# Attention scores with the rotary keys' two halves stacked, and softmax scaling moved into the transposing matmul

## The chip, the cores and the metric

The kernel runs on one core of a Trainium2 chip. The metric is the device time of one execution in microseconds, given as the median of several runs. Five engines work side by side: TensorE (PE; its weight loads are listed apart as PEld), VectorE (DVE), ScalarE (ACT), GpSimd (POOL) and SyncE (SP, which here only issues transfers). TensorE writes to PSUM, where eight banks of 128 partitions by 512 fp32 values are used in turn; DVE and ACT read them out.

## The reference

Two layers run over 256 latent and 256 context tokens with 1024 features. Each layer has a SwiGLU feed-forward block, a token mixer and a second feed-forward block. The mixer of the first layer is a short convolution, that of the second is multi-head latent attention, and only that one is touched here:

```python
def latent_attention(q, k_all, v_all):        # 8 heads, 256 latent queries, 512 keys
    ...
def softmax_attend(q, k, v):
    s = jnp.einsum("bhqd,bhkd->bhqk", q, k).astype(jnp.float32) * QK_SCALE
    p = jax.nn.softmax(s, axis=-1).astype(v.dtype)
    return jnp.einsum("bhqk,bhkd->bhqd", p, v)
```

Queries and keys have 192 features in each head: 128 plain ones ("nope") and 64 rotary ones, which carry a rotation by position. The rotary part of a key is the same for all heads but for a factor of the head's normalisation.

## The kernel before

All activations and weights are fp32. To multiply with nearly full precision, each operand is split into a rounded high part (type fp32r, made on ACT by a cast, `split`, L210) and a low part (the rest, made on DVE by a subtraction, L211), and a product takes three matmuls: high by high, high by low, low by high. The helper `mm3` (L200 to L202) does this for the weights. In the attention stage the names are `q` and `qr` for the plain and the rotary queries (views of the tiles `arh` and `arl`, high and low, which also hold the transposed compressed queries `cqT` and the compressed keys `ckT`), `kt` for a pair of heads' keys (a pair of tiles `wh`, `wl` from the pool of weight slots), `pts` for transposed probabilities (also `wh`, `wl`), `vv` for the values (`vyh`, `vyl`) and `ot` for the output.

The code is traced in a program order, and a scheduler then fixes one static instruction list for each engine. Each engine works through its list in order, with semaphores between engines. The attention stage's program order comes from a hand-written string of steps (`MLA_ORDER`) and then a loop over i = 0 to 15 (8 heads by 2 blocks of 128 queries). The parts that matter:

- `q_norm`, `q_out` (steps N and O, once for each block of 128 tokens): the rotation of the queries in rows (`rot`, on DVE and POOL), then transposes on TensorE (L874) of three tiles of 128 by 512: two with the plain parts of four heads each, `tn`, and one with the rotary parts of all eight heads, `tr`. Two heads' rotary parts share a 128-wide transpose, so a head's 64 rotary features land on partitions 0 to 63 or 64 to 127. Each transposed tile is split by ACT and DVE (L210, L213 on ACT; L211, L214 on DVE).
- `kv_mm` (L916 to L918): compressed keys times the weights `kv`, for keys (step K) and values (step V). `k_pair` normalises the keys and writes plain parts to `kn` (DVE, L940) and rotary parts to `h` (POOL, L945).
- `keys(j)` for heads 2j and 2j+1: 12 transposes on TensorE (L997), eight of `kn` and four of `h`, and three splits.
- `scores(i)`: six matmuls into one PSUM bank, three over 128 plain features (L1012 to L1014) and three over 64 rotary features (L1015 to L1017, 64 rows of the array); then the row maximum on DVE (L1020), the exponential with a row sum on ACT (L1023), the reciprocal on DVE (L1024), and on DVE the scaling of the 128 by 512 probabilities `p` (L1025).
- `probs(i)`: four transposes of `p` (L1035) against the unit matrix (`cst`), and a split.
- `values(hd)`: twelve matmuls (L1046 to L1048) and a split to `ot`.

In the loop, `scores` runs two steps ahead of `probs`, and `keys` for the next pair of heads stands three steps ahead of its first use. A transpose is one pass through the array; a normal matmul of fp32 operands (not fp32r) takes two, each with its own weight load, and shows as two instructions in the profile. The normalisation's `norm_stats` (L361, L362) and the first layer's `mod_rows` (L284) already use such fp32 matmuls; L284 places four of them side by side in the columns of the array (`tile_position`, 32 columns each). The output projection's weights are converted (`conv_raw`, L178 on ACT and L179 on DVE) during the last steps of the loop.

```python
def split(self, src, h, l, scale=None):
    if scale is None:
        self.nc.scalar.copy(h, src)                                              # L210, ACT
        self.nc.vector.tensor_tensor(l, src, h.bitcast(F32), ALU.subtract)       # L211, DVE
```

Of the kernel before, what the change touches and what calls it, by code (L numbers as in the profile page):

```python
# [15 lines left out]
P = 128  # L16
# [60 lines left out]
class Kern:  # L77
# [578 lines left out]
    def sumsq(self, src, nh, w, out, scale=1.0):  # L656
        nc = self.nc
        for i in range(nh):
            j = self.tmp.tile([P, T], F32, tag="t2", name=self.nm("sj"), bufs=1)
            nc.scalar.activation(  # L660
                j[:, :w], src[:, i * w:(i + 1) * w], AF.Square, scale=scale, accum_out=out[:, i:i + 1]
            )
# [14 lines left out]
    def mla(self, l, nxt, mp):  # L677
# [9 lines left out]
        qr = [t[:, nq:nq + nq // 2].rearrange("p (h t) -> p h t", h=HEADS // 2) for t in (arh, arl)]  # L687
        b = nq + nq // 2
        cqT = [t[:, b:b + 2 * NLAT].rearrange("p (k t) -> p k t", k=2) for t in (arh, arl)]
        ckT = [t[:, b + 2 * NLAT:b + 2 * NLAT + T] for t in (arh, arl)]  # L690
        kn = mp.tile([P, 4, HEADS * P], F32, tag="kn", name="kn")
        krr = self.cst[:, P:].rearrange("p (t r) -> p t r", t=4)
# [163 lines left out]
        def q_norm(tt):  # L856
# [10 lines left out]
            return src[:1] + [(t, qr, 0, None)] + src[1:]  # L867

        def q_out(tt, src):
            ts = slice(tt * P, (tt + 1) * P)  # L870
            for t, dst, h0, g in src:
                tp = self.mmps()
                for i in range(4):
                    nc.tensor.transpose(tp[:, i * P:(i + 1) * P], t[:, i * P:(i + 1) * P], self.ident)  # L874
# [111 lines left out]
        kts, pts, ps = {}, {}, {}  # L986

        def keys(j):
            kts[j] = kt = self.wslot()
            for i in range(3):  # L990
                tp = self.mmps()
                for tt in range(4):
                    if i < 2:
                        src = kn[:, tt, (2 * j + i) * P:(2 * j + i + 1) * P]
                    else:
                        src = self.h[:, 2 * tt + j // 2, NLAT + (j % 2) * P:NLAT + (j % 2 + 1) * P]
                    nc.tensor.transpose(tp[:, tt * P:(tt + 1) * P], src, self.ident)  # L997
                s = slice(i * T, (i + 1) * T)
                self.split(tp, kt[0][:, s], kt[1][:, s])

        def scores(i):
# [3 lines left out]
            sl = slice(e * hp, (e + 1) * hp)  # L1005
            ns = slice(e * T, (e + 1) * T)
            rs = slice(2 * T, 3 * T)
# [3 lines left out]
            qp = [t[sl, j, qs] for t in qr]  # L1011
# [3 lines left out]
            mm(S, qp[0], kt[0][sl, rs], start=False, stop=False)  # L1015
            mm(S, qp[0], kt[1][sl, rs], start=False, stop=False)  # L1016
            mm(S, qp[1], kt[0][sl, rs], start=False, stop=True)  # L1017
# [7 lines left out]
            nc.vector.tensor_scalar(p, p, st[:, 2:3], None, ALU.mult)  # L1025
# [341 lines left out]
```

## Time and profile before

| | |
|---|---|
| median of 3 runs | 1633.65 us (1632.89 to 1637.13) |
| the profiled execution's own time, and its span | 1631.98 us, 1630.2 us |
| TensorE busy | 1599.2 us (98%), 8747 matmuls |
| DVE busy, ACT busy, POOL busy | 1113.4 us (68%), 586.1 us (36%), 58.6 us (4%) |
| transfers | 245.32 MB, mean 150 GB/s |
| attention stage | about 1288 to 1413 us of the span |

How to read it: the timeline has a row for each run of like instructions, with the start in the span, the time from the first start to the last end, engine, line, operation, the tiles (output and inputs), the shape and the count; in brackets stands the idle time before it and who ended that. Matmuls are pipelined, so one starts before the last has ended: what a matmul costs on TensorE is the distance from its start to the next one's start, not its own duration. The list of waits gives who waited for whom, total us, how often, and the longest.

### The profile page before, as it was taken

The page shows a single profiled execution, that of the slowest core. Times are in us where ns is not written, and L with a number is a line of the kernel's source. Part 1 is how long each engine was busy: PE and PEld are TensorE (multiplying, and loading weights), DVE is VectorE, ACT ScalarE, POOL GpSimd, SP SyncE. Part 2 cuts the span into 40 slices and gives each one's busy share as a digit, 9 for nine tenths or more (in the row PEclk, how much of TensorE's full clock was granted, in tenths as well). Part 3 has the DMA queues.
Part 4 walks back from the last instruction along what each step waited for, and adds up shares of the span by engine and source line. Part 5 has one row for each costly group of instructions (what it writes and reads, how often), then busy time and mean ns, then how long its engine had stood idle before and what let it go on. Part 6 is the DMA issues. An engine that isn't in the chain of part 4 may idle for free.

```text
span 1630.2 us, 21844 instructions
## 1 busy us (share of the span) xinstructions
PE 1599.2 (98%) x8747; PEld 1374.0 (84%) x8747; DVE 1113.4 (68%) x1967; ACT 586.1 (36%) x915; POOL 58.6 (4%) x69
## 2 busy tenths in 40 slices
PE   5999999999999999999999999999999998999999
PEld 4888888889888898888888898888888976899999
DVE  4568666676897678766666677767665678885553
ACT  4622222224423352222232352132223465664442
POOL 0000000001000200000000200000000211000000
PEclk9999999999999999999999999999999999999999
DMA  9545444431354425444444425444432120245553
GB/s 361 187 158 194 161 161 168 167 143 67 140 194 169 154 78 183 166 165 146 181 149 148 143 80 191 161 159 160 166 142 102 61 78 1 82 174 200 181 193 104
DMA packets 48677, 245.32 MB, mean 150 GB/s; under 512 B 5440, under 2 KB 6720, under 8 KB 33216
## 3 DMA queue, kind: packets, MB, share of 16 engines
q1 hardware_dynamic: 48576, 243.94, 41.6%
q8 instruction: 68, 1.11, 0.3%
q14 instruction: 33, 0.27, 0.1%
HBM read 242.87 MB, written 1.05 MB: 150 GB/s over the span
## 4 chain that ended last, share of the span: by engine, by line
PE 93%; DVE 4%; ACT 1%; DMA 1%; issue 0%; SPq 0%; POOL 0%; DVEq 0%; ACTq 0%
PE mm L200 30%; PE mm L202 30%; PE mm L201 29%; DVE nt L378 0%; PE mm L1035 0%; PE mm L1015 0%; DMA h<-hT 0%; PE mm L284 0%; PE mm L1046 0%; DMA raw<-wukv 0%; DVE nu L383 0%; DVE yl L384 0%; PE mm L1047 0%; PE mm L1016 0%; PE mm L1048 0%
## 5 line engine op out<-in xcount | busy, mean ns | idle before, releaser
L200 PE MATMUL mm<-yh,wh 128*128 128x512 f32 (+1 forms) x1674 | 596.7, 357 | 4.6 <-ACT wh L1209 2.5
L201 PE MATMUL mm<-yh,wl 128*128 128x512 f32 (+1 forms) x1674 | 595.2, 356 | 0.4 <-DVE wl L1211 0.3
L202 PE MATMUL mm<-yl,wh 128*128 128x512 f32 (+1 forms) x1674 | 594.3, 356 | 0.1
L178 ACT CAST wh<-raw 128x1024 fp32r<-128x1024 f32 (+4 forms) x348 | 319.1, 941 | 617.7 <-PE mm L202 508.4
L179 DVE TENSOR_TENSOR wl<-raw,wh 128x1024 fp32r<-128x1024 f32 (+4 forms) x348 | 377.6, 1103 | 47.1 <-ACT wh L178 45.3
L200 PEld LDWEIGHTS mm<-yh,wh 128*128 128x128 f32 x1674 | 316.6, 189 | 51.4 <-ACT yh L382 3.1
L201 PEld LDWEIGHTS mm<-yh,wl 128*128 128x128 f32 x1674 | 316.8, 189 | 45.3 <-DVE wl L1211 0.9
L202 PEld LDWEIGHTS mm<-yl,wh 128*128 128x128 f32 x1674 | 316.1, 189 | 45.2 <-DVE yl L384 0.3
L260 DVE CUSTOM_DVE_ANT_0 junk<-wm,crow 128x1024 f32<-128x1024 f32 x256 | 316.0, 1234 | 3.9
L200 PE MATMUL mm<-gh,wh 128*128 128x512 f32 (+1 forms) x848 | 294.9, 348 | 0.0
L202 PE MATMUL mm<-gl,wh 128*128 128x512 f32 (+1 forms) x848 | 294.4, 347 | 0.0
L201 PE MATMUL mm<-gh,wl 128*128 128x512 f32 (+1 forms) x848 | 294.2, 347 | 0.0
L455 DVE TENSOR_TENSOR s<-mm,s 128x512 f32<-128x512 f32 (+1 forms) x86 | 54.1, 629 | 249.7 <-PE mm L202 240.8
L202 PEld LDWEIGHTS mm<-gl,wh 128*128 128x128 f32 x848 | 160.5, 189 | 20.5 <-DVE gl L211 0.5
L200 PEld LDWEIGHTS mm<-gh,wh 128*128 128x128 f32 x848 | 160.5, 189 | 20.2
L201 PEld LDWEIGHTS mm<-gh,wl 128*128 128x128 f32 x848 | 160.5, 189 | 20.2
L402 DVE SCALAR_TENSOR_TENSOR h<-mm,fin,h 128x256 f32<-128x256 f32 x192 | 88.7, 478 | 122.7 <-PE mm L202 122.7
L454 ACT ACTIVATE s<-mm 128x512 f32<-128x512 f32 (+1 forms) x86 | 47.2, 548 | 189.9 <-PE mm L202 189.7
L211 DVE TENSOR_TENSOR gl<-s,gh 128x512 fp32r<-128x512 f32 (+1 forms) x86 | 53.5, 622 | 2.1 <-ACT gh L210 2.1
L210 ACT CAST gh<-s 128x512 fp32r<-128x512 f32 (+1 forms) x86 | 48.7, 566 | 6.5 <-DVE s L455 6.5
L346 ACT ACTIVATE sq<-h 128x256 f32<-128x256 f32 (+1 forms) x50 | 25.4, 507 | 69.9 <-DVE h L402 68.3
L382 ACT ACTIVATE yh<-nt,fin 128x256 fp32r<-128x256 f32 x66 | 36.5, 595 | 33.7 <-DVE nt L378 31.9
(215 smaller groups left out, 962.5 us busy)
## 6 DMA issues: line engine op xcount, KB each, us to landing
raw<-w SPq DMA_DIRECT2D x101, 1024.0 KB, 4.8
wm<-wmod SPq DMA_DIRECT2D x132, 512.0 KB, 3.7
raw<-w SPq DMA_DIRECT2D x32, 896.0 KB, 4.6
raw<-cin_cu SPq DMA_DIRECT2D x8, 1024.0 KB, 4.8
early<-wmod SPq DMA_DIRECT2D x12, 512.0 KB, 8.9
raw<-cin_b SPq DMA_DIRECT2D x8, 512.0 KB, 3.5
raw<-cout SPq DMA_DIRECT2D x4, 1024.0 KB, 4.8
raw<-wo SPq DMA_DIRECT2D x4, 1024.0 KB, 4.9
```

The lines of the kernel that those rows point to most:

```text
L178: self.nc.scalar.copy(h[:, b0:b1], raw[:, b0:b1])
L179: self.nc.vector.tensor_tensor(l[:, b0:b1], raw[:, b0:b1], h[:, b0:b1].bitcast(F32), ALU.subtract)
L200: mm(o, wh[:, b], xh[:, k, c[0]:c[1]], start=start, stop=False)
L201: mm(o, wl[:, b], xh[:, k, c[0]:c[1]], start=False, stop=False)
L202: mm(o, wh[:, b], xl[:, k, c[0]:c[1]], start=False, stop=stop)
L210: self.nc.scalar.copy(h, src)
L211: self.nc.vector.tensor_tensor(l, src, h.bitcast(F32), ALU.subtract)
L260: ins = nc.vector.tensor_tensor_reduce(junk, w, self.crow[:, cond, :], 1.0, 0.0, ALU.mult, ALU.add, o)
L382: nc.scalar.activation(yh, t, AF.Identity, bias=sh, scale=a)
L402: self.nc.vector.scalar_tensor_tensor(hh, ps[:, lo:hi], self.f(l, j, d, cond), hh, ALU.mult, ALU.add)
L454: nc.scalar.activation(s[:, :w], p1[:, :w], AF.Silu)
L455: nc.vector.tensor_tensor(s[:, :w], p3[:, :w], s[:, :w], ALU.mult)
```

## The change

- Keys: for each head its own tile of rotary keys is made, with the high part on partitions 0 to 63 and the low part on partitions 64 to 127. To have the same 64 features on both halves of the partitions, `keys` no longer transposes `h`: the new helper `twice` multiplies a 64-column piece with the unit matrix two times, into partitions 0 to 63 and into 64 to 127, as two normal fp32 matmuls placed in the two halves of the array's columns. ACT casts the whole tile, and DVE overwrites its lower half by the rest.
- Queries: `q_out` doubles each head's rotary part over both halves in the same way. The doubled `qr` takes twice the room in `arh` and `arl`; `cqT` lies in its last part, and `ckT` moves to two scratch tiles (tags `t2` and `t3`).
- Scores: two rotary matmuls over 128 rows in place of three over 64 rows.
- Softmax: DVE no longer scales `p`. ACT multiplies the unit matrix by the reciprocals to a diagonal matrix `diag`, and `probs` multiplies `p` with `diag` in a normal fp32 matmul in place of a transpose against the unit matrix, so that transposing and scaling are one.
- The junk tiles of `sumsq` move from tag `t2` to `sq`.

```diff
@@ mla
-        qr = [t[:, nq:nq + nq // 2].rearrange("p (h t) -> p h t", h=HEADS // 2) for t in (arh, arl)]
-        b = nq + nq // 2
-        cqT = [t[:, b:b + 2 * NLAT].rearrange("p (k t) -> p k t", k=2) for t in (arh, arl)]
-        ckT = [t[:, b + 2 * NLAT:b + 2 * NLAT + T] for t in (arh, arl)]
+        qr = [t[:, nq:2 * nq].rearrange("p (h t) -> p h t", h=HEADS) for t in (arh, arl)]
+        cqT = [t[:, 2 * nq - 2 * NLAT:2 * nq].rearrange("p (k t) -> p k t", k=2) for t in (arh, arl)]
+        ckT = [self.tmp.tile([P, T], F32R, tag="t2", name="ckh", bufs=1),
+               self.tmp.tile([P, T], F32R, tag="t3", name="ckl")]
@@ q_norm, q_out
-            return src[:1] + [(t, qr, 0, None)] + src[1:]
+            return src[:1] + [(t, qr, 0, None), (t, qr, 4, None)] + src[1:]
+        def twice(out, t):
+            for c in (0, QK_ROPE):
+                mm(out[c:c + QK_ROPE], t, self.ident, start=True, stop=True, tile_position=(0, c))
...
+                    if dst is qr:
+                        twice(tp[:, i * P:(i + 1) * P], t[:, (h0 + i) * QK_ROPE:(h0 + i + 1) * QK_ROPE])
+                    else:
+                        nc.tensor.transpose(tp[:, i * P:(i + 1) * P], t[:, i * P:(i + 1) * P], self.ident)
@@ keys
-            for i in range(3):
+            for i in range(4):
...
+                        c = NLAT + (j % 2) * P + (i - 2) * hp
+                        twice(o, self.h[:, 2 * tt + j // 2, c:c + hp])
...
+                    hl = kt[i - 2][:, 2 * T:3 * T]
+                    nc.scalar.copy(hl, tp)
+                    nc.vector.tensor_tensor(hl[hp:P], tp[hp:P], hl[hp:P].bitcast(F32), ALU.subtract)
@@ scores
-            mm(S, qp[0], kt[0][sl, rs], start=False, stop=False)
-            mm(S, qp[0], kt[1][sl, rs], start=False, stop=False)
-            mm(S, qp[1], kt[0][sl, rs], start=False, stop=True)
+            mm(S, qp[0], hl, start=False, stop=False)
+            mm(S, qp[1], hl, start=False, stop=True)
...
-            nc.vector.tensor_scalar(p, p, st[:, 2:3], None, ALU.mult)
+            nc.scalar.activation(diag[:, i % 4], self.ident, AF.Copy, scale=st[:, 2:3])
@@ probs
-                nc.tensor.transpose(tp[:, t * P:(t + 1) * P], p[:, t * P:(t + 1) * P], self.ident)
+                mm(tp[:, t * P:(t + 1) * P], p[:, t * P:(t + 1) * P], diag[:, i % 4], start=True, stop=True)
```

The instruction lists of SP and POOL keep their order; those of PE, DVE and ACT change within the attention stage, from the first `q_out` on for PE. On PE, at `keys(2)` in the loop, the list of before reads as follows (`mm` is a PSUM bank; a row is one instruction, or as many as the count at its end; lines 1005, 872, 1027 to 1031 and 1049 of the changed kernel hold what lines 997, 997, 1012 to 1017 and 1035 hold before):

```order
L997 MATMUL mm_10788<-cst,kn 128x128
L997 MATMUL mm_10795<-cst,kn 128x128 x4
L997 MATMUL mm_10802<-cst,h 128x128 x4
L1012 MATMUL mm_10809<-wh_10647,arh 128x512
L1013 MATMUL mm_10809<-wl_10648,arh 128x512
L1014 MATMUL mm_10809<-wh_10647,arl 128x512
L1015 MATMUL mm_10809<-wh_10647,arh 128x512
L1016 MATMUL mm_10809<-wl_10648,arh 128x512
L1017 MATMUL mm_10809<-wh_10647,arl 128x512
L1035 MATMUL mm_10823<-cst,p_10734 128x128 x4
```

The same place on PE after the change:

```order
L1005 MATMUL mm_10844<-cst,kn 128x128 x4
L1005 MATMUL mm_10851<-cst,kn 128x128 x4
L872 MATMUL mm_10858<-cst,h 64x128 x8
L872 MATMUL mm_10869<-cst,h 64x128 x8
L1027 MATMUL mm_10880<-wh_10692,arh 128x512
L1028 MATMUL mm_10880<-wl_10693,arh 128x512
L1029 MATMUL mm_10880<-wh_10692,arl 128x512
L1030 MATMUL mm_10880<-wl_10693,arh 128x512
L1031 MATMUL mm_10880<-wl_10693,arl 128x512
L1049 MATMUL mm_10893<-diag,p_10791 128x128 x4
```

Four transposes of `h` have become sixteen 64-column matmuls in two banks rather than one, the rotary part of a score has two rows rather than three, and the four transposes of `p` have become four matmuls with `diag`.

On PE, at the second `q_out` among the products of compressed keys with weights, the list of before reads:

```order
L916 MATMUL mm_10437<-kv_9968,arh 128x512
L917 MATMUL mm_10437<-kv_9969,arh 128x512
L916 MATMUL mm_10444<-kv_9968,arh 128x512
L917 MATMUL mm_10444<-kv_9969,arh 128x512
L874 MATMUL mm_10466<-cst,tn_10342 128x128 x4
L874 MATMUL mm_10473<-cst,tr_10346 128x128 x4
L874 MATMUL mm_10480<-cst,tn_10344 128x128 x4
L918 MATMUL mm_10437<-kv_9968,arl 128x512
L918 MATMUL mm_10444<-kv_9968,arl 128x512
```

The same place on PE after the change (lines 924 to 926 are before's 916 to 918, line 882 before's 874):

```order
L924 MATMUL mm_10455<-kv_9970,ckh 128x512
L925 MATMUL mm_10455<-kv_9971,ckh 128x512
L924 MATMUL mm_10462<-kv_9970,ckh 128x512
L925 MATMUL mm_10462<-kv_9971,ckh 128x512
L882 MATMUL mm_10484<-cst,tn_10345 128x128 x4
L872 MATMUL mm_10491<-cst,tr_10349 64x128 x8
L872 MATMUL mm_10502<-cst,tr_10349 64x128 x3
L926 MATMUL mm_10455<-kv_9970,ckl 128x512
L926 MATMUL mm_10462<-kv_9970,ckl 128x512
L872 MATMUL mm_10502<-cst,tr_10349 64x128 x5
L882 MATMUL mm_10513<-cst,tn_10347 128x128 x4
```

Four transposes of the rotary queries have become sixteen 64-column matmuls in two banks, broken once by two products with the low part of the compressed keys, which before stood behind all the transposes.

On ACT, at the conversion of the last weights but one in the loop, the list of before reads:

```order
L1023 ACTIVATE p_11041,st_11042<-mm_11034,st_11042,rq_10207 128x512
L210 CAST ot_10622<-mm_11048 128x256
L210 CAST wh_11063<-mm_11065 128x4x128
L178 CAST wh_11163<-raw_9974 128x1024
L210 CAST wh_11063<-mm_11086 128x4x128
L178 CAST wh_11163<-raw_9974 128x1024
L210 CAST wh_11063<-mm_11108 128x4x128
```

The same place on ACT after the change (line 1037 is the exponential, line 1039 the diagonal matrix):

```order
L1037 ACTIVATE p_11119,st_11120<-mm_11113,st_11120,rq_10210 128x512
L1039 ACTIVATE diag<-cst,st_11120 128x128
L210 CAST ot_10668<-mm_11126 128x256
L210 CAST wh_11141<-mm_11143 128x4x128
L178 CAST wh_11240<-raw_9976 128x1024 x2
L210 CAST wh_11141<-mm_11163 128x4x128
L1037 ACTIVATE p_11156,st_11157<-mm_11150,st_11157,rq_10338 128x512
```

The two conversions now stand one behind the other, ahead of a cast of probabilities that stood between them, and the diagonal matrix follows its exponential directly.

More of the change, by code (lines that the diff above doesn't have):

```diff
@@ L658, in sumsq @@
         for i in range(nh):
-            j = self.tmp.tile([P, T], F32, tag="t2", name=self.nm("sj"), bufs=1)
+            j = self.tmp.tile([P, T], F32, tag="sq", name=self.nm("sj"))
             nc.scalar.activation(
@@ L873, in q_out @@
                 for i in range(4):
-                    nc.tensor.transpose(tp[:, i * P:(i + 1) * P], t[:, i * P:(i + 1) * P], self.ident)
+                    if dst is qr:
+                        twice(tp[:, i * P:(i + 1) * P], t[:, (h0 + i) * QK_ROPE:(h0 + i + 1) * QK_ROPE])
+                    else:
+                        nc.tensor.transpose(tp[:, i * P:(i + 1) * P], t[:, i * P:(i + 1) * P], self.ident)
                 self.split(
@@ L986, in mla @@
         kts, pts, ps = {}, {}, {}
+        diag = self.tmp.tile([P, 4, P], F32, tag="rstd", name="diag")
         def keys(j):
             kts[j] = kt = self.wslot()
-            for i in range(3):
+            for i in range(4):
                 tp = self.mmps()
                 for tt in range(4):
+                    o = tp[:, tt * P:(tt + 1) * P]
                     if i < 2:
                         src = kn[:, tt, (2 * j + i) * P:(2 * j + i + 1) * P]
+                        nc.tensor.transpose(o, src, self.ident)
                     else:
[L996 to L999, printed above, removed]
+                        c = NLAT + (j % 2) * P + (i - 2) * hp
+                        twice(o, self.h[:, 2 * tt + j // 2, c:c + hp])
+                if i < 2:
+                    s = slice(i * T, (i + 1) * T)
+                    self.split(tp, kt[0][:, s], kt[1][:, s])
+                else:
+                    hl = kt[i - 2][:, 2 * T:3 * T]
+                    nc.scalar.copy(hl, tp)
+                    nc.vector.tensor_tensor(hl[hp:P], tp[hp:P], hl[hp:P].bitcast(F32), ALU.subtract)
         def scores(i):
@@ L1004, in scores @@
             kt = kts[j]
-            sl = slice(e * hp, (e + 1) * hp)
             ns = slice(e * T, (e + 1) * T)
-            rs = slice(2 * T, 3 * T)
             qs = slice(qb * P, (qb + 1) * P)
@@ L1010, in scores @@
             qn = [t[:, hd, qs] for t in q]
-            qp = [t[sl, j, qs] for t in qr]
+            qp = [t[:, hd, qs] for t in qr]
+            hl = kt[e][:, 2 * T:3 * T]
             mm(S, qn[0], kt[0][:, ns], start=True, stop=False)
```

## The prediction

> **What bounds the kernel.** I read the page first, for the engine that carries the span, then the attention stage by windows, then who waits for whom in it, and last the timeline for the price of each kind of matmul. Of the page, the busy times, two rows of the forty slices and the chain that ended last:
>
> ```profile
> PE 1599.2 (98%) x8747; PEld 1374.0 (84%) x8747; DVE 1113.4 (68%) x1967; ACT 586.1 (36%) x915; POOL 58.6 (4%) x69
> PE   5999999999999999999999999999999998999999
> PEclk9999999999999999999999999999999999999999
> PE 93%; DVE 4%; ACT 1%; DMA 1%; issue 0%; SPq 0%; POOL 0%; DVEq 0%; ACTq 0%
> ```
>
> TensorE is busy nearly everywhere at a full clock, and the chain lies on it for 93%. Behind the start only one slice is below 9: the 34th (1345 to 1386 us), in the attention stage, the only one that the change touches. Windows over that stage (busy us of each engine; the first column is the length):
>
> ```profile
> 1333.00:1353.30 20.30, 15.58 (x75) 10.05 (x73) 19.04 (x55) 15.34 (x42) 3.82 (x6) 1.00 0.00 1
> 1353.30:1364.90 11.60, 10.09 (x46) 6.92 (x47) 9.54 (x26) 7.05 (x17) 1.13 (x2) 1.00 0.00 0
> 1364.90:1413.00 48.10, 46.41 (x275) 34.94 (x274) 40.84 (x97) 28.68 (x61) 1.24 (x3) 1.00 0.09 27
> ```
>
> The columns behind the length are PE, PEld, DVE, ACT, POOL. In the first stretch (`q_out`, `kv_mm`, `keys(0)`) DVE is the fuller engine, 19.0 of 20.3 us, and TensorE idles 4.7 us. In the second (first scores, last `k_pair`, `keys(1)`) TensorE idles 1.5 us, in the loop 1.7 of 48.1 us: there its own work sets the pace. TensorE's waits from 1333 to 1414 us (us in total, times, longest):
>
> ```profile
> PE mm L997 <- DVE kn L940: 1.5, 1, 1.5
> PE mm L916 <- DVE arl L214: 1.5, 2, 0.8
> PE mm L916 <- ACT arh L213: 1.1, 1, 1.1
> PE mm L1046 <- ACT wh L210: 1.0, 1, 1.0
> PE mm L1035 <- DVE p L1025: 0.6, 1, 0.6
> PE mm L1012 <- ACT wh L210: 0.6, 1, 0.6
> ```
>
> Few and short waits, each for a split or a scaling on DVE or ACT. So the sum is made on TensorE first, and then asks what of it fills idle time.
>
> **Scores: three 64-row matmuls become two of 128 rows.** One score in the timeline, and the transposes of `p` behind it (start, duration, instruction):
>
> ```profile
> 1364.90 0.47 PE L1012 MATMUL mm<-wh,arh 128*128 128x512 f32 x1
> 1365.22 0.39 PE L1013 MATMUL mm<-wl,arh 128*128 128x512 f32 x1
> 1365.44 0.40 PE L1014 MATMUL mm<-wh,arl 128*128 128x512 f32 x1
> 1365.77 0.49 PE L1015 MATMUL mm<-wh,arh 64*128 64x512 f32 x1
> 1366.11 0.39 PE L1016 MATMUL mm<-wl,arh 64*128 64x512 f32 x1
> 1366.34 0.39 PE L1017 MATMUL mm<-wh,arl 64*128 64x512 f32 x1
> 1366.66 0.66 PE L1035 MATMUL mm<-cst,p 128*128 128x128 f32 x4
> 1367.07 0.47 PE L1012 MATMUL mm<-wh,arh 128*128 128x512 f32 x1
> ```
>
> From start to start a full 512-column matmul costs 0.22 to 0.23 us (1365.22 to 1365.44). Going into the 64-row form costs 0.33, its second one 0.34, and leaving it 0.32: each change of form adds about 0.1 us on one or two steps. From the start of L1014 to the transposes it is 1.22 us; with two full-row matmuls it is 3 x 0.23 = 0.69. Saved: 0.53 us, times 16 scores, **-8.5 us**.
>
> **Probabilities: transposes become normal fp32 matmuls.** Transposes in a run, and after a matmul of another kind:
>
> ```profile
> 1361.97 1.04 PE L997 MATMUL mm<-cst,kn 128*128 128x128 f32 x8
> 1368.36 0.38 PE L1046 MATMUL mm<-wh,vyh 128*128 128x256 f32 x1
> 1368.58 0.60 PE L1035 MATMUL mm<-cst,p 128*128 128x128 f32 x4
> ```
>
> Eight take 1.04 us and four 0.60, so each further one costs 0.11, and a lone one lasts 0.60 - 0.33 = 0.27. For normal fp32 matmuls with 128 rows and columns, `norm_stats` is the nearest (each line is one matmul call, two passes of 256 columns):
>
> ```profile
> 1438.75 0.28 PE L202 MATMUL mm<-z,wh 128*128 128x258 f32 x1
> 1438.87 0.60 PE L361 MATMUL mm<-acc,ones 128*128 128x256 f32 x2
> 1439.30 0.59 PE L362 MATMUL mm<-sq,ones 128*128 128x256 f32 x2
> 1439.55 0.47 PE L200 MATMUL mm<-z,wh 128*128 128x258 f32 x1
> ```
>
> One call costs 0.43 us for 256 columns, so about 0.22 for 128, twice a transpose: 64 x 0.11 = **+7.0 us**. Lower bound 0.11 each (one pass, no change), upper 0.43 (no gain from half the columns). I take the half, since the passes of the next row cost 0.11 at 128 columns. The step into L361 is an ordinary 0.12, whereas a transpose behind L1046 starts 0.22 behind it (0.12 is usual for 256 columns) and the first one behind a score costs 0.06 more (0.66 against 0.60): 16 such entries go, about **-1.2 us**.
>
> **Doubled rotary parts.** `mod_rows` runs four fp32 matmuls side by side in the array's columns, 32 of them in two passes each, 64 rows of the profile:
>
> ```profile
> 38.00 0.39 PE L201 MATMUL mm<-yh,wl 128*128 128x512 f32 x1
> 38.23 0.40 PE L202 MATMUL mm<-yl,wh 128*128 128x512 f32 x1
> 38.56 1.95 PE L284 MATMUL mm<-wm,cTp 128*32 128x128 f32 x64
> 40.44 0.50 PE L200 MATMUL mm<-yh,wh 128*128 128x512 f32 x1
> 40.78 0.39 PE L201 MATMUL mm<-yh,wl 128*128 128x512 f32 x1
> ```
>
> (1.95 - 0.27) / 15 = 0.11 us for each of 16 groups: matmuls in different columns overlap fully, and a group pays two passes, 0.22 us. So a call of `twice` (two halves of the columns) costs 0.22. There are 8 calls in each `q_out` and each `keys`, 6 x 8 = 48 of them, 10.6 us, in place of 6 x 4 transposes at 0.11, 2.6 us: **+7.9 us** (one call at 0.11 would give +2.6, at 0.44, with no overlap, +18.5). The form changes too: 0.33 in place of 0.23 on entering L284, and 0.34 on the second step after it, with about 0.1 at the first: 0.3 for each of six blocks, three more breaks of blocks (one in the second `q_out`, two in `keys(0)`, where the last rows of `h` come late) and 0.1 for each of the three `kn` transposes in the loop, which no longer follow transposes: **+3.0 us** (0 to 4).
>
> TensorE's sum is -8.5 + 7.0 - 1.2 + 7.9 + 3.0 = +8.2 us.
>
> **What the rest adds, and what covers.** The other engines' prices, from groups of the loop's window and from the copy of a 128 by 128 row tile:
>
> ```profile
> L1025 DVE TENSOR_SCALAR p<-p,st 128x512 f32<-128x512 f32 x14 | 6.8, 483 | 0.1
> L211 DVE TENSOR_TENSOR wl<-mm,wh 128x512 fp32r<-128x512 f32 x24 | 16.0, 683 | 0.9 <-ACT wh L210 0.5
> L210 ACT CAST wh<-mm 128x512 fp32r<-128x512 f32 x21 | 11.9, 590 | 8.2 <-PE mm L1035 7.9
> L178 ACT CAST wh<-raw 128x1024 fp32r<-128x1024 f32 x4 | 4.2, 1049 | 1.0 <-PE mm L1017 1.0
> L292 ACT COPY row<-mm x5: 255/260/266, 17.6 to 51.4; 128x128 f32<-128x128 f32 x3, 64x128 f32<-64x128 f32 x2
> ```
>
> - DVE loses 16 scalings at 0.48 us, 7.7 us. It gains two splits in `q_out` and one extra subtraction in each `keys` (half the partitions, the same 512 columns, so taken at the full 0.68): 6 x 0.68 = 4.1 us.
> - ACT gains six casts, 3.5 us, and 16 diagonal matrices at 0.26, 4.2 us: 28.7 of 48.1 us in the loop becomes about 34. It stays below TensorE. But a diagonal stands behind its own exponential and waits for DVE's reciprocal, so ACT's queue (casts of probabilities, keys, outputs) stands for that long. The two-step lead of `scores` covers it.
> - First stretch: TensorE's part of the sum there is two `q_out` and `keys(0)`, 3 x 1.3 us, and 1.8 us of form changes, 5.7 us: 15.6 + 5.7 = 21.3 us. DVE has 19.0 + 2 x 0.68 = 20.4. Both are about the length of 20.3, so the stretch grows by 1.0 at the least; two engines that wait for each other do not interlock without gaps, and the products with `ckl` come behind four banks' worth of the others. I take +2.5, so **-3.2 us** of the sum is covered (0 to -4.7, the idle time).
> - Second stretch: the 1.5 us wait for `kn` on DVE has two scalings in front of it in DVE's queue, 1.0 us, which go. **-1.3 us** (0 to -1.5).
> - The 0.6 us wait for the scaled `p` (L1025) goes: **-0.6 us**.
> - The 1.0 us wait of L1046 for a cast of probabilities is ACT's: two weight conversions of 1.05 stand around it. In the new order both stand ahead of that cast: **+1.0 us** (0 to +2).
> - `keys` takes four PSUM banks at once rather than three, and its last cast comes later. Three steps of lead cover it; without that, a bank's wait is about a split, 0.6 to 0.7 us, three times: 0 to +2, taken as 0.
> - `sumsq`'s other tag moves one chain later on ACT, ahead of the first `q_out`; its transpose on TensorE stands more than a microsecond later: 0.
>
> 8.2 - 3.2 - 1.3 - 0.6 + 1.0 = **+4.1 us**. The sum is made against the profiled execution, 1631.98 us (span 1630.2 and 1.8 around it), which lies 1.7 under the median of 1633.65; I add it to the median: **1637.7 us**, +0.25%. About 0.3% (4.9 us) is what a measurement of this kernel tells from no change.
>
> **The rivals.**
> 1. *Slower: nothing covers.* If ACT's waits for reciprocals, in a queue that also frees PSUM banks, hold TensorE as often as DVE's scalings did, and the first stretch takes TensorE's 5.7 us whole, the sum is 8.2 + 1.0 and up to 2 for banks: +9 to +11, 1643 to 1645. For it: the stretch before the loop already has two full engines. Against: DVE gets 3.6 us net, and the loop's waits are rare. It decides from a reciprocal that reaches ACT more than one step of `scores` late.
> 2. *All idle time is used:* 8.2 - 4.7 - 1.5 - 0.6 = +1.4, 1635. Against: the rows of waits are for splits that the change adds to.
> 3. *The two halves of `twice` do not overlap* (a 64-column form is nowhere in this trace): 48 x 0.22 = +10.6 on top, about 1648. Against: L284 with four column places.
> 4. *Faster: an fp32 matmul of 128 columns costs one transpose.* Then +7.0 and +5.3 of the 7.9 vanish: 4.1 - 12.3 = -8, about 1625. Against: every L284 and L361 call shows as two instructions, each at its own step.
> 5. *Faster: a transpose is dearer than its steps show.* If each of the 88 transposes that go (64 of `p`, 24 rotary ones) held the array for its whole 0.27 us, they would take 23.8 us now, against 14.1 + 10.6 after: +0.9 in place of 14.9, and the total -9.9, about 1624. Against: eight transposes in 1.04 us.
>
> [...]
>
> **How the numbers follow.** Forecast (partial cover, +1.5 to +5): 0.45. First rival, and what lies between it and the forecast: 0.33. Second 0.07, third 0.07, fourth 0.04, fifth 0.04. The forecast's own range is 1635 to 1639. The range of 8 in 10 leaves out the third and the faster two and reaches from a little under the second (no change less the spread of three runs) to the end of the first: 1632 to 1645. Slower by over 0.3%: 0.33, 0.07 and a little of the forecast, 0.42; faster 0.08; within 0.50.
>
> **What would show it.** Two full-row matmuls on L1030 and L1031 at 0.23 a step; L1049 in eight instructions for a head's block at 0.11; L872 in pairs that start together, a pair each 0.11, 1.8 us for sixteen calls; fewer waits for DVE and some for ACT `diag` or `wh`; TensorE about 8 us busier. It is wrong if L872's pairs start one after the other, if L1049 steps at 0.2 or more, or if TensorE waits for `diag` in most steps of the loop.

## The result, and the profile after

| | before | after |
|---|---|---|
| median of the runs | 1633.65 us (1632.26 to 1637.13, 5 runs) | 1643.69 us (1641.70 to 1645.12, 5 runs) |
| profiled execution, its span | 1631.98 us, 1630.2 us | 1643.69 us, 1641.9 us |
| TensorE busy | 1599.2 us, 8747 matmuls | 1609.6 us, 8963 matmuls |
| DVE, ACT busy | 1113.4 us, 586.1 us | 1112.0 us, 594.6 us |

The changed kernel is slower: ratio 1.0054, 95% interval 1.0038 to 1.0069. The prediction was 1637.7 us with a range of 1632 to 1645. The time lies in the range, but 6 us above the forecast, where the first rival ("nothing covers", 1643 to 1645) had put it.

The page of the changed kernel looks like the one before: the same shares, TensorE 10 us busier.

```profile
PE 1609.6 (98%) x8963; PEld 1391.1 (85%) x8963; DVE 1112.0 (68%) x1957; ACT 594.6 (36%) x937; POOL 58.5 (4%) x69
PE   5999999999999999999999999999999989999999
PEclk9999999999999999999999999999999999999999
PE 93%; DVE 4%; ACT 2%; DMA 1%; issue 0%; SPq 0%; POOL 0%; DVEq 0%; ACTq 0%
```

Only the stage tells more. Both kernels' traces are cut into three parts at the same four places: the first transposes of `q_out`, the first score, the first product with `p` (transposes before, `diag` after), and the last one of these. The columns are start and end, length, busy us of PE, PEld, DVE, ACT and POOL with their instructions, the granted clock, and two columns of the transfers. Before:

```profile
1332.91:1353.33 20.42, 15.67 (x76) 10.14 (x74) 19.16 (x55) 15.37 (x42) 3.82 (x6) 1.00 0.00 1
1353.33:1361.48 8.15, 8.15 (x31) 5.22 (x31) 6.20 (x16) 3.90 (x11) 0.00 (x0) 1.00 0.00 0
1361.48:1412.75 51.27, 48.10 (x287) 36.39 (x287) 44.15 (x106) 31.80 (x68) 2.37 (x4) 1.00 0.08 24
```

After:

```profile
1335.47:1361.10 25.63, 21.45 (x161) 15.65 (x159) 21.24 (x59) 16.67 (x44) 3.80 (x6) 0.93 0.00 1
1361.10:1368.26 7.16, 6.51 (x28) 4.99 (x28) 6.78 (x15) 4.59 (x11) 0.00 (x0) 1.00 0.00 0
1368.26:1424.16 55.90, 53.02 (x421) 47.17 (x421) 40.33 (x96) 37.83 (x87) 2.38 (x4) 1.00 0.11 39
```

The first stretch grows by 5.2 us, the second shrinks by 1.0, the loop grows by 4.6. TensorE is busier by 4.9 us in the loop, and in the first stretch by 5.8, but there the clock column says 0.93. Ahead of the first stretch another 1.25 us is lost (a wait, below), and 1.3 us of the two spans' difference of 11.7 lies in their first 31 us, where both kernels execute the same list. TensorE's waits in the stage after the change:

```profile
PE mm L1060 <- ACT wh L210: 2.1, 3, 1.3
PE mm L924 <- DVE r L651: 1.6, 1, 1.6
PE mm L1049 <- ACT diag L1039: 1.4, 2, 0.8
PE mm L789 <- DVE ta L781: 1.3, 1, 1.3
PE mm L924 <- DVE rz L636: 0.9, 1, 0.9
PE mm L872 <- DVE r L652: 0.7, 1, 0.7
```

The waits for `kn` (1.5), for the scaled `p` (0.6) and that of `kv_mm` for `arl` (1.5) are gone by name; in their places stand waits for `diag` and for `ta`, a longer one for ACT's casts of probabilities (2.1 rather than 1.0), and two of `kv_mm` (L924). The one of 1.6 us is put down to a small root on DVE, but the work that ended just ahead of it (1340.49) was the split `arl` of the first `q_out` (L214), which frees a PSUM bank. I take that bank for the cause; the trace does not name it.

The clock of 0.93 is one stretch of half speed, 3.41 us long. Three windows of that length in the changed kernel's first stretch, in the columns used above:

```profile
1339.24:1342.65 3.41, 1.40 (x6) 0.84 (x6) 3.01 (x9) 2.77 (x7) 0.00 (x0) 1.00 0.00 0
1342.65:1346.07 3.42, 3.16 (x8) 2.48 (x9) 2.70 (x6) 1.47 (x4) 1.43 (x2) 0.50 0.00 0
1346.07:1349.48 3.41, 2.76 (x16) 2.11 (x16) 2.78 (x9) 2.85 (x7) 0.00 (x0) 1.00 0.00 0
```

TensorE is busy for only 1.40 of 3.41 us, and in the next 3.41 us it runs at half clock: a 512-column step that takes 0.23 us takes 0.43. About half of the 3.16 busy us, 1.6, is lost (an estimate from the clock of 0.50). Before the change the three emptiest windows of the stage look like this one, and nothing follows:

```profile
1360.90:1364.31 3.41, 2.11 (x15) 1.48 (x13) 3.24 (x11) 3.11 (x8) 0.54 (x1) 1.00 0.00 0
```

### The profile page after: what moved, and what is told of

It is laid out like the page before. It is cut to its first block, busy times and chain, and to the rows that moved or that the text cites. A ratio compares the mean times of both kernels' runs of the same rounds, so it can differ in the third digit from the quotient of the medians.

```text
span 1641.9 us, 22295 instructions
## 1 busy us (share of the span) xinstructions
PE 1609.6 (98%) x8963; PEld 1391.1 (85%) x8963; DVE 1112.0 (68%) x1957; ACT 594.6 (36%) x937; POOL 58.5 (4%) x69
## 4 chain that ended last, share of the span: by engine, by line
PE 93%; DVE 4%; ACT 2%; DMA 1%; issue 0%; SPq 0%; POOL 0%; DVEq 0%; ACTq 0%
PE mm L200 29%; PE mm L201 29%; PE mm L202 29%; PE mm L1049 1%; PE mm L872 1%; DVE nt L378 0%; ACT wh L178 0%; DMA h<-hT 0%; PE mm L284 0%; PE mm L1060 0%; DMA raw<-wukv 0%; DVE nu L383 0%; DVE yl L384 0%; PE mm L1061 0%; PE mm L1062 0%
```

## The experiments

Each has five rounds on one chip; the kernel before lay at 1633.2 to 1633.6 us in all of them. "Clock" is the mean granted clock, averaged over a kernel's runs.

| | median us (range, runs) | ratio to before, 95% interval | clock |
|---|---|---|---|
| before | 1633.33 (95 runs of all sets) | | 0.9980 |
| after | 1643.69 (1641.70 to 1645.12, 5) | 1.0054 [1.0038, 1.0069] | 0.9974 |
| e1, only the tag of `sumsq` | 1637.01 (1634.42 to 1638.84, 9) | 1.0019 [1.0009, 1.0028] | 0.9973 |
| e2, e1 and `ckT` in scratch | 1638.30 (1635.32 to 1641.21, 11) | 1.0027 [1.0018, 1.0036] | 0.9968 |
| e3, after without `diag` | 1637.23 (1635.35 to 1639.45, 10) | 1.0022 [1.0013, 1.0031] | 0.9974 |
| e4, before with `diag` | 1647.92 (1639.74 to 1649.46, 6) | 1.0079 [1.0062, 1.0097] | 0.9947 |
| e5, after, junk in place | 1643.54 (1640.50 to 1644.89, 8) | 1.0048 [1.0028, 1.0068] | 0.9969 |
| e6, after, keys by a shift | 1640.09 (1637.65 to 1642.54, 12) | 1.0031 [1.0017, 1.0045] | 0.9968 |
| e7, only what pays | 1635.97 (1633.72 to 1640.04, 12) | 1.0013 [0.9999, 1.0027] | 0.9961 |
| e8, after, 12 useless transposes | 1640.34 (1637.32 to 1643.85, 12) | 1.0038 [1.0024, 1.0052] | 0.9982 |
| e9, e7, half of the scaling on ACT | 1637.40 (1634.73 to 1638.55, 11) | 1.0021 [1.0012, 1.0031] | 0.9957 |
| e10, after, `diag` on DVE | 1641.37 (1640.49 to 1643.02, 5) | 1.0050 [1.0037, 1.0062] | 0.9978 |
| e11, e9, 16 useless transposes | 1634.09 (1631.87 to 1638.49, 11) | 1.0003 [0.9994, 1.0012] | 0.9976 |
| e12, e7, 64 useless transposes | 1637.09 (1635.73 to 1641.40, 12) | 1.0024 [1.0014, 1.0033] | 0.9971 |

How much longer each part of the stage is than before, in the profiled executions (us, from the starts of the same instructions; the first column runs from the stage's first product with `arh`, L848 in both kernels, to the first transposes of `q_out`):

| | to the first `q_out` | first stretch | second | loop |
|---|---|---|---|---|
| after | 1.25 | 5.21 | -0.99 | 4.63 |
| e3 | 1.25 | 6.19 | -0.36 | -1.79 |
| e4 | 1.22 | 0.11 | 1.06 | 6.76 |
| e5 | 1.23 | 5.54 | -0.99 | 4.59 |
| e6 | 1.25 | 4.09 | 0.59 | 1.46 |
| e7 | -0.30 | 2.82 | -0.47 | -0.46 |
| e8 | 1.25 | 2.17 | -0.94 | 4.61 |
| e9 | -0.31 | 4.33 | 1.11 | -2.60 |
| e10 | 1.25 | 5.06 | -0.57 | 3.40 |
| e11 | 1.24 | 2.82 | 0.92 | -2.60 |
| e12 | -0.29 | 2.82 | -0.27 | 0.12 |

Some of these entries hold a half-clock window, which comes and goes between runs: first stretch of after, e3 (two windows), e5, e6, e9 and e10; second of e4, e6, e9 and e11; loop of e7 and e12. The first column is 1.3 us of waiting in after, e3, e6, e8 and e10, but a half-clock window in e4, e5 and e11. That window follows a wait of 1.3 to 1.6 us for the first split of the queries, which is no effect of an edit: e9 and e11 have the same list up to there, and only e11's profile shows it.

### The two small moves: e1 and e2

```diff
@@ sumsq
-            j = self.tmp.tile([P, T], F32, tag="t2", name=self.nm("sj"), bufs=1)
+            j = self.tmp.tile([P, T], F32, tag="sq", name=self.nm("sj"))
```

> The kernel before with one line of the change alone: the junk tiles of sumsq in tag sq rather than t2. The theory that the change's cost is partly in its scratch moves expects +1.3 us (about 1635): TensorE waits 1.3 us for the tile ta on L789, as in the changed kernel, and the shift stays to the end. The rival, that the prediction was right to cost it at nothing and that the whole +10 us lies in the new matmuls, expects no change (within 0.5 us) and no such wait.

e1 is slower by 0.19%. Its trace has the changed kernel's wait for `ta`, which the trace of before has not:

```profile
1329.07 0.33 PE L789 MATMUL mm<-cst,ta 128*128 128x128 f32 x1 [1.31 <-DVE ta L781]
```

With the tag `t2`, ACT's list has the sum of squares for this `ta` ahead of five other ACT instructions of 0.5 to 0.6 us (three squares of queries, L667, two copies, L863); with `sq` it stands behind them. So the moved scratch tile costs 1.25 us by itself, and not 0. The ratio makes 3.1 us of it; the rest goes with a lower clock, since e1's three runs at 0.998 average 1634.8 us and the 51 runs of before at 0.998 average 1633.8.

e2 adds this to e1:

```diff
-    ckT = [t[:, b + 2 * NLAT:b + 2 * NLAT + T] for t in (arh, arl)]
+    ckT = [self.tmp.tile([P, T], F32R, tag="t2", name="ckh", bufs=1),
+           self.tmp.tile([P, T], F32R, tag="t3", name="ckl")]
```

> The kernel before with the scratch moves alone: sumsq in tag sq, and the compressed keys ckT in the tags t2 and t3; transposes, scores and scaling stay. If the late low part of the compressed keys (behind the rotation's scratch in the same tag) costs time of its own, +2.5 to +4 us (about 1637), with TensorE waiting on L916 or L918 until about 1.5 us later than before. If the doubled queries' matmuls would have covered that wait anyhow, still +1.3 us more than nothing here; if only the sumsq line counts, +1.3 us (1635).

Ratio 1.0027 against 1.0019: the intervals overlap, and the scratch of `ckT` is not shown to cost anything. In its profile the first stretch is 2.0 us longer than before, but a half-clock window lies in it.

### The two halves: e3 and e4

e3 is the changed kernel with `p` scaled on DVE and transposed as before; e4 is the kernel before with `diag`:

```diff
-    nc.vector.tensor_scalar(p, p, st[:, 2:3], None, ALU.mult)
+    nc.scalar.activation(diag[:, i % 4], self.ident, AF.Copy, scale=st[:, 2:3])
...
-    nc.tensor.transpose(tp[:, t * P:(t + 1) * P], p[:, t * P:(t + 1) * P], self.ident)
+    mm(tp[:, t * P:(t + 1) * P], p[:, t * P:(t + 1) * P], diag[:, i % 4], start=True, stop=True)
```

> The changed kernel without the diagonal matrix: probabilities are scaled on DVE and transposed as before; stacked keys, doubled queries, two rotary matmuls and the scratch moves stay. By TensorE's prices -8.5 + 7.9 + 3.0 = +2.4 us, and with the scratch moves +1.3 to +3: +4 to +5 us (1637.5 to 1638.5). The rival, that TensorE's sum is covered and the change's cost is the waits for diag on ACT, expects this kernel within 1.5 us of before.

> The kernel before with the diagonal matrix alone: probabilities are transposed and scaled by a normal fp32 matmul with diag, everything else stays. By TensorE's prices 64 x 0.11 - 1.2 = +5.8 us, less DVE's relief of 1.0 to 1.5 us: +4.5 us (1638). If the waits for diag on ACT come on top, +6. The rival, that a busier TensorE is covered by its idle time in the loop, expects +1.5 to +2.5 us, the waits for diag alone.

Each half alone is slower than before. In the loop e3 gains 1.8 us and e4 loses 6.8; together that is 5.0, and the changed kernel loses 4.6. So the loop's loss is `diag`'s, and it is what its matmuls cost: in e4's loop TensorE is busy for 55.44 of 58.03 us, before for 48.10 of 51.27, so its idle time is no longer than before. What e3 loses lies in the first stretch. e3's time is just under its expectation (1637.5 to 1638.5), e4's is 10 us above its own (1638). e4's median is above the changed kernel's, though it changes less: its mean clock is 0.9947, and one of its runs at 0.999 took 1639.74 us.

### The order on ACT: e5

```diff
@@ sumsq
-            j = self.tmp.tile([P, T], F32, tag="sq", name=self.nm("sj"))
...
+        self.nc.scalar.activation(j, src[:, :w], AF.Square, scale=scale, accum_out=out[:, 0:1])
@@ its two callers
+            self.sumsq(p, w, st, t[:, 0:w], w ** -0.5)
...
+            self.sumsq(kr, QK_ROPE, sskr[:, tt:tt + 1], krr[:, tt, :])
```

> The changed kernel, but the junk of sumsq goes into the tile that is overwritten right behind it (`ta`, `krr`), so that its tag `sq` takes no part. On ACT the cast of the first `q_out` (`arh`) then stands ahead of the second sum of squares again, as it does before the change; in the changed kernel it stands behind both sums and two roots. Theory A (the moved junk costs, through ACT's order): the 1.3 us wait of L789 for `ta` goes (-1.25), the 1.6 us wait of L924 for a bank that the late `arh`/`arl` splits free goes in part (-1 to -2), and with the idle time the half-clock window behind it: 1639.5 to 1641, -2.5 to -4. Theory B (the first stretch is slow because DVE and TensorE are both full there, whatever the order): only the 1.25 goes or nothing, 1642.4 to 1643.7.

The wait for `ta` is gone and the wait for the bank is 0.4 us rather than 1.6, as theory A has it. The time did not follow. TensorE now waits in one piece, a little later, for the second half of the compressed keys:

```profile
PE mm L919 <- ACT ckh L213: 2.0, 1, 2.0
1344.79:1348.20 3.41, 1.37 (x6) 0.81 (x5) 3.41 (x9) 2.44 (x7) 0.00 (x0) 1.00 0.00 0
1348.20:1351.62 3.42, 3.42 (x15) 2.08 (x15) 2.00 (x6) 1.22 (x3) 1.18 (x2) 0.50 0.00 0
```

DVE is busy for the whole of the window in which TensorE waits, and the half-clock window follows again. Theory A fell: the wait that was removed here came back as another. That DVE is full there fits this, and is not tested by itself.

### Keys without `twice`: e6

```diff
@@ keys: one bank and 4 transposes, not two banks and 8 calls
-                        twice(o, self.h[:, 2 * tt + j // 2, c:c + hp])
...
+                        nc.tensor.transpose(o, self.h[:, 2 * tt + j // 2, c:c + P], self.ident)
...
+                    for e in range(2):
+                        hl = kt[e][:, 2 * T:3 * T]
+                        s, o = slice(e * hp, (e + 1) * hp), slice((1 - e) * hp, (2 - e) * hp)
+                        nc.scalar.copy(hl[s], tp[s])
+                        nc.vector.tensor_tensor(hl[o], tp[s], hl[s].bitcast(F32), ALU.subtract)
```

> The changed kernel, but `keys` transposes `h` four times as before the change, and ACT and DVE stack the halves by writing to the other half of the partitions (two half-height casts and two half-height subtractions each in place of one cast and one subtraction of two banks). TensorE loses 32 calls of `twice` at 0.22 and gains 16 transposes at 0.11: -5.3, and 0.3 of form change for each of four blocks: -1.2; one bank less per call. Theory A (TensorE's own steps are what the change costs outside the first stretch): three of four `keys` count whole, the first in part: -5 to -6.5, 1637 to 1639. Theory B (the casts and subtractions on ACT and DVE, and waits for them, cost as much): within 2 us of the changed kernel, 1642 to 1645.

1640.09, 3.6 below the changed kernel: between the theories, nearer to A. TensorE's busy time in the loop falls from 53.02 to 48.62 us, 4.4 for three `keys`, where the prices give 4.9 (three quarters of 5.3 and 1.2); the price of `twice` holds.

### Only what pays: e7 and e9

e7 keeps the stacked scores and the doubled queries, and has e6's keys, e5's scratch and no `diag`.

> Only what pays by the prices so far: scores with stacked halves (two rotary matmuls for three, -8.5), queries doubled by `twice` (16 calls at 0.22 for 8 transposes at 0.11, +2.6, and 0.8 of form changes), keys stacked by shifting partitions on ACT and DVE, junk of sumsq in place, and the probabilities scaled on DVE and transposed as before the change. TensorE's sum is -5.1 us. Theory A: it counts but for 1 to 2 us of new waits in the first stretch: 1629 to 1631, -2 to -4 against before. Theory B (the first stretch takes back all: two more splits there and one more cast and subtraction in each `keys`, with half-clock windows behind the idle time): 1632 to 1635, no change or a little slower.

1635.97: theory B, or a little worse. TensorE's busy time in the three parts falls from 71.9 to 68.9 us in spite of a half-clock window, but its idle time rises from 7.9 to 12.8. First stretch and loop of e7, and the two windows around the fall of the clock:

```profile
1332.73:1355.97 23.24, 18.71 (x132) 12.95 (x130) 21.30 (x58) 16.30 (x44) 3.80 (x6) 1.00 0.00 1
1363.65:1414.45 50.80, 43.67 (x273) 36.88 (x273) 45.06 (x110) 32.19 (x69) 2.37 (x4) 0.97 0.12 42
1405.30:1408.71 3.41, 1.25 (x9) 1.01 (x9) 3.05 (x9) 3.25 (x7) 0.00 (x0) 1.00 0.63 259
1408.71:1412.12 3.41, 3.41 (x19) 3.41 (x18) 2.74 (x6) 0.96 (x2) 0.00 (x0) 0.50 0.31 77
```

DVE is now busier than TensorE in the loop, TensorE waits 5.1 us in the stage for `p` and its reciprocals, and the clock falls in the loop. The first stretch is 2.82 us longer than before, and no half-clock window lies in it. e9 moves every second scaling to ACT:

> The version of e7 (stacked halves, keys stacked by a shift, probabilities scaled and transposed), with the scaling of `p` for every second score moved from DVE to ACT. In e7 DVE is busy for 45.0 of the loop's 50.8 us and TensorE waits there 5.1 us for `p` and its reciprocals, once so closely that a half-clock window follows; ACT is busy for 32.2. DVE loses 8 scalings of 0.48 (-3.9), ACT gains 8 of about 0.6 (+4.7). Theory A (DVE sets e7's loop): the waits for `p` fall by 2 to 4 us and the half-clock windows become rarer: 1631 to 1634, about 3 below e7 and 0 to 2 below the kernel before. Theory B (the chain from score to probability is what is late, on whatever engine): within 1 us of e7, 1635 to 1637.

Its time is no better than e7's (1637.40 us, on another chip) and above both theories' ranges, with the lowest mean clock of all. First stretch and loop of its profile:

```profile
1332.69:1357.44 24.75, 20.22 (x133) 14.05 (x131) 21.30 (x58) 16.29 (x44) 3.81 (x6) 0.93 0.00 1
1366.69:1415.36 48.67, 42.74 (x272) 35.18 (x273) 42.96 (x102) 37.28 (x77) 2.37 (x4) 1.00 0.11 40
```

The waits for `p` fall from 5.1 to 3.8 us (2.6 of them for the `p` that ACT scales), and those for ACT's casts grow from 1.5 to 1.9. The loop is 2.1 us shorter than e7's, of which about 1.7 are e7's half-clock window (half of 3.41), and 2.6 shorter than before. So the loop moved a little the way of theory A, and the time is lost elsewhere; that the chain from score to probability is what comes late is not shown.

Up to the first score e7 and e9 execute the same lists on TensorE, DVE and ACT, and in both TensorE waits 2.0 us for `ckh`. In e7 the wait lies across two windows, TensorE is busy for 0.51 of the emptier one, and full clock follows; in e9 the windows lie a little otherwise, the one that holds the wait has 0.42, and half clock follows. The stretch takes 23.24 and 24.75 us: one half-clock window costs 1.5 us.

### Useless work against the falling clock: e8, e11, e12

e8 repeats the last transposes of the first `q_out`, e11 puts transposes of the unit matrix ahead of the product that waits for `ckh`:

```diff
@@ e8, in q_out
+                if tt == 0 and t is src[-1][0]:
+                    for i in range(12):
+                        c = slice(i % 4 * P, (i % 4 + 1) * P)
+                        nc.tensor.transpose(tp[:, c], t[:, c], self.ident)
@@ e11, in kv_mm
+            if (tt, piece) == (2, 0):
+                for i in range(16):
+                    nc.tensor.transpose(p[:, 0:P], self.ident, self.ident)
```

> The changed kernel with useless work where TensorE waits: the last four transposes of the first `q_out` are done three times more (12 matmuls of 0.11, +1.3 us of TensorE work, same values to the same bank). Ahead of the half-clock window at 1342.7 TensorE stands idle for 1.6 us of 3.4. Theory A (the clock falls after a 3.4 us window in which TensorE is busy for less than about 0.6, so useless work keeps it up): the half-clock window at this place is gone, the runs' mean clocks are 0.998 to 0.999 rather than 0.996 to 0.999, and the time is 0 to 2 us lower than the changed kernel's, 1641.5 to 1643.5, in spite of more work. Theory B (the clock has nothing to do with the idle time): the half-clock windows stay as frequent, and the time is as the changed kernel's or up to 1.3 us above it, 1643.5 to 1645.

> e9 with useless work where e7's TensorE stands for 2.0 us waiting for the high part of the compressed keys (`ckh`), ahead of the first product of tokens 256 to 383: 16 transposes of the unit matrix into the bank that this product fills next (1.8 us of TensorE work). Theory A (the clock falls after a window with too little work): the clock stays up there and the time is 0 to 2 us below e9. Theory B (such a place is rare enough in e9, or the filling delays the product): the same as e9 to 1 us slower.

Both are faster with more work: e8 by 3.35 us against the changed kernel (the intervals of the two ratios overlap), e11 by 3.3 us against e9 on the same chip, where one interval ends at 1.0012 and the other begins there. e11 is the cleaner test also because its lists on TensorE, ACT and DVE are those of e9 but for the 16 transposes (in e8 a few products change places). The same place in both timelines, e9 first:

```profile
1344.20 0.80 PE L919 MATMUL mm<-kv,ckh 128*128 128x512 f32 x1 [2.04 <-ACT ckh L213]
1344.79 0.63 PE L920 MATMUL mm<-kv,ckh 128*128 128x512 f32 x1
1345.22 0.63 PE L919 MATMUL mm<-kv,ckh 128*128 128x512 f32 x1
1345.64 0.63 PE L920 MATMUL mm<-kv,ckh 128*128 128x512 f32 x1
```

```profile
1345.06 1.91 PE L921 MATMUL mm<-cst 128*128 128x128 f32 x16
1347.27 0.51 PE L922 MATMUL mm<-kv,ckh 128*128 128x512 f32 x1 [0.30 <-ACT ckh L213]
1347.61 0.40 PE L923 MATMUL mm<-kv,ckh 128*128 128x512 f32 x1
1347.84 0.40 PE L922 MATMUL mm<-kv,ckh 128*128 128x512 f32 x1
1348.08 0.39 PE L923 MATMUL mm<-kv,ckh 128*128 128x512 f32 x1
```

The product waits for `ckh` in both, but behind the useless transposes the steps are 0.24, not 0.43. The same windows, e9 and then e11:

```profile
1340.74:1344.15 3.41, 1.42 (x7) 0.82 (x5) 3.41 (x9) 3.41 (x9) 0.17 (x1) 1.00 0.00 0
1344.15:1347.56 3.41, 3.36 (x13) 2.56 (x14) 3.08 (x8) 0.49 (x2) 1.19 (x2) 0.50 0.00 0
1344.94:1348.35 3.41, 3.11 (x23) 2.55 (x22) 3.41 (x9) 2.37 (x7) 0.00 (x0) 1.00 0.00 0
```

The first stretch of e11 takes 23.24 us with 1.8 us of useless work in it, e9's 24.75. (The two profiled executions as a whole do not show the gain, since e11's has the half-clock window ahead of the stage that e9's has not.) At equal mean clock e11's runs lie between 1.3 us below and 1.1 us above e9's, so its gain is that more of them keep a high clock. At equal mean clock e8's are still 0.6 to 2.7 us below the changed kernel's (few runs), so e8's gain is not the clock's alone. That the clock falls behind idle time, and that this costs time, is shown by these profiles (e9: TensorE busy for 1.42 of 3.41 us, then a clock of 0.50 and the longer stretch; e11: 3.21 and 3.11 of 3.41 us, and full-clock steps behind, four transposes in 0.60 us); how much a filling gains is less sure, as the intervals meet. e12 fills six places of e7:

> The version of e7 with useless transposes of the unit matrix at each of its longer waits: 16 ahead of the product that waits for `ckh` (as in e11), 8, 12, 4 and 12 ahead of the transposes of `p` that wait (steps 0, 3, 8 and 13), and 12 ahead of the last values: 64 in all, 7.0 us of TensorE work, in about 8.5 us of waiting. The scheduler puts some other work of the loop in another order for it. Theory A (e7 loses by its clock, 0.996 in the mean of its runs, what it saves in work): the mean clock rises to 0.998 or more and the time falls to 1632 to 1634, no more than the kernel before. Theory B (the filling delays real work as much as it helps): as e7, 1635 to 1637, or slower.

Theory B: 1637.09. The filling changed the scheduler's order in the loop, the last values then waited 2.40 us for ACT's cast, and the clock fell there. No version beat the kernel before; the intervals of e7 and e11 hold a ratio of 1.

### The diagonal on DVE: e10

```diff
-    nc.scalar.activation(diag[:, i % 4], self.ident, AF.Copy, scale=st[:, 2:3])
+    nc.vector.tensor_scalar(diag[:, i % 4], self.ident, st[:, 2:3], None, ALU.mult)
```

> The changed kernel with `diag` made by DVE, right behind its reciprocal, rather than by ACT. TensorE's work is the same. The wait of L1049 for `diag` is 1.4 us and that of L1060 for ACT's cast of probabilities 2.1 us in the changed kernel's trace, 1.0 us for the latter before the change. Theory A (ACT's queue stands still at each diagonal matrix until DVE's reciprocal has come, and its casts come later for that): both waits shrink, by 1 to 2.5 us together, 1641 to 1642.7. Theory B (the chain from score to probability is simply as long on either engine, or DVE, with 4.3 us more, is late with its own splits): 1643 to 1646.

1641.37 lies in theory A's range, the loop is 1.2 us shorter than the changed kernel's, and L1060's wait falls from 2.1 to 1.7 us; L1049 still waits 1.1 us, at the first probabilities. The ratios' intervals overlap, so the loop's trace points to theory A and the times do not settle it. The diagonals' prices, ACT's in the changed kernel's loop and DVE's in e10's:

```profile
L1039 ACT ACTIVATE diag<-cst,st 128x128 f32<-128x128 f32 x15 | 6.0, 407 | 1.9 <-DVE st L1038 1.8
L1039 DVE TENSOR_SCALAR diag<-cst,st 128x128 f32<-128x128 f32 x16 | 4.5, 283 | 0.2
```

## Why the prediction was right or wrong

**TensorE's prices were right.** The changed kernel's timeline around the second step of the loop:

```profile
1370.22 1.97 PE L872 MATMUL mm<-cst,h 128*64 128x128 f32 x32
1372.12 0.50 PE L1027 MATMUL mm<-wh,arh 128*128 128x512 f32 x1
1372.45 0.39 PE L1028 MATMUL mm<-wl,arh 128*128 128x512 f32 x1
1372.69 0.39 PE L1029 MATMUL mm<-wh,arl 128*128 128x512 f32 x1
1372.92 0.40 PE L1030 MATMUL mm<-wl,arh 128*128 128x512 f32 x1
1373.15 0.39 PE L1031 MATMUL mm<-wl,arl 128*128 128x512 f32 x1
1373.38 1.05 PE L1049 MATMUL mm<-diag,p 128*128 128x128 f32 x8
1374.19 0.47 PE L1027 MATMUL mm<-wh,arh 128*128 128x512 f32 x1
```

Thirty-two passes of `twice` take 1.9 us, so the halves overlap and a call costs 0.22 with its two passes; the rotary rows of a score step by 0.23; the eight passes of one `probs` take 0.81 from start to next start, 0.1 each (L1049 shows 128 matmuls and 128 weight loads for its 64 calls, L1035 before the change 64 of each for 64). The third and fourth rivals fall by these rows. The fifth falls by the result: had each transpose held the array for its whole 0.27 us, the change would have been faster (an estimate of 1624 us, from 88 transposes at 0.27); it is slower, and the step of 0.11 is what transposes cost here. Their step does go by the granted clock: four take 0.60 us at full clock (e11) and 1.06 in e9's half-clock window.

**The loop.** In these parts of the stage the prediction's terms give: 13 scores -6.9, probabilities +7.0 - 1.2, three `keys` with `twice` +4.0 and form changes +1.2, conversions +1.0, waits for L1025 and `kn` -0.6 and -1.3, +3.2 in all. Measured: +4.63. The waits for L1025 and `kn` went as predicted, and L1060's wait grew by 1.1 for the predicted 1.0. New is the wait for `diag`, 0.76 us of it in this part, which the prediction had covered by the two-step lead. The diagonals also cost ACT 0.41 us each, not 0.26. The rest is in shares of half a us that I did not tell apart.

**The second part** shrank by 0.99; three scores at 0.53 are 1.6, and the other 0.65 us of waiting for `diag` stands here.

**`sumsq`'s tag, a term put at 0, was mis-sized:** +1.25 us, shown by e1. The prediction saw that its sum moves later on ACT, and trusted the distance to its transpose; the transpose waited 1.3 us.

**The first stretch, a term put at +2.5, measured +5.21. This is the step that failed most.** The prediction let two full engines cover 3.2 of TensorE's 5.7 us. TensorE's work there grew by less: 21.45 us, less 1.6 for the half-clock window, is 19.9, +4.2. But its idle time stayed, 4.75 us before and 4.2 after, so only 0.6 us was covered. Then the idle time, gathered into one window, brought half clock, for 1.6 us. e8, where that window is filled and the order differs a little, grows by 2.17, near the prediction's 2.5. Its first stretch:

```profile
1333.68:1356.28 22.60, 20.56 (x173) 15.70 (x171) 21.11 (x59) 16.34 (x44) 3.80 (x6) 1.00 0.00 1
```

TensorE has 4.9 us more work there than before, 1.2 of it useless, and only 2.0 us of idle time, so 2.7 us are covered at full clock. e7 has 3.0 us more work there, also at full clock, and grows by 2.8: next to nothing is covered. So the cover that the prediction took was possible, but fullness of the engines does not settle how much comes of it. What in e8's order makes the difference stays open; e5 shows that a mere change of the order on ACT does not help.

So the sum of 4.1 became 10.1 in the stage (1.25 + 5.21 - 0.99 + 4.63). The first rival had the size right, 9 to 11, from TensorE's work without cover, and for the loop its reason (ACT waits for reciprocals) is in the trace with 1.4 us. But it had no falling clock in its sum, and without the half-clock window the stage would have lost about 1.6 us less; part of its agreement is luck.

## What the runs showed of the hardware that was not expected

In these profiles the granted clock went with TensorE's work in the 3.41 us before. In every profile the stretches of full and half clock behind the start, but for the last one, which the end cuts off, last whole multiples of 3.41 us (changed kernel: 1310.72 us, that is 384 of them, then 3.41, then 296.96). Of all such windows at full clock from 30 to 1440 us in the 14 profiles, those with TensorE busy for less than half were followed by half clock in 10 of 10 cases, those from 0.5 to 0.6 in 4 of 10, from 0.6 to 0.7 in 5 of 32, and the fuller ones never (144 of them, counting the 14 emptiest windows of each profile). The busy column flatters a matmul that stands alone: a lone transpose lasts 0.27 us and its step is 0.11. Counted at steps (0.11 us for 128 or 192 columns, 0.12 for 256, 0.23 for 512), all 17 windows below 0.4 were followed by half clock, and of the fuller ones two (0.48 in e2, 0.49 in e1). The longest single gap in a window behind which the clock fell was 0.3 to 2.4 us. No long gap was needed: a wait of 1.6 us with a few shorter ones around it was enough in the changed kernel, and in the five windows of 0.6 to 0.7 that half clock followed no gap was longer than 0.6 us.

The windows lie at other places of the span in each profile: the edge that begins the long stretch of full clock is at 29.7 us before the change, at 31.9 after it, and between 29.4 and 33.0 in the 14 profiles, a spread of a whole window. So the same idle time falls into one window in one run and into two in the next, as in e9 (0.42 busy, then half clock) and e7 (0.51, then full clock). The scatter of the times goes with the clock: over 95 runs of the kernel before, the mean time is 1632.6 us at a mean clock of 0.999 (33 runs), 1633.8 at 0.998 (51), 1635.7 at 0.997 (3), 1638.0 at 0.996 (2), 1640.7 at 0.994 (3) and 1642.0 at 0.993 (3). That the place of the windows is what differs between these runs is not seen, since they left no trace.

## What to carry to other kernels

On an engine that is 98% busy, price a change first by its steps on that engine, and do not count on cover where two engines are both nearly full: the same stretch covered 0.2 us of 3.0 in one list and 2.7 of 4.9 in another, both at full clock. Here, idle time of TensorE that was gathered within one window of 3.41 us cost about 1.5 us more in the next one (23.24 and 24.75 us for the same stretch in e7 and e9), so look at the clock by windows, and at the mean clock beside each time, before a difference of some us is explained by instructions. A scratch tile that changed its tag changed the order of a static list (1.25 us in e1), and the first reader of what moved is where its price stood.
